# Layer 0 of a two-layer encoder trunk: recurrence products over 65 columns and rows, solves of two head pairs at once, heads in turn, another order

## Chip, cores and metric

The kernel runs on one core of one Trainium2 chip. The metric is the time of one execution in microseconds of the device: the median of three runs.

## The reference, cut to what matters

512 tokens of 1024 features pass two layers. Layer 0 projects the normed input once and feeds a convolution branch (31 taps per channel, then a layer norm) and a branch of 16 heads with a recurrence; both are gated, joined and projected. Layer 1 is a sparse attention with 16 heads. The change is in layer 0. Per head and token:

```
sa    = state @ (-kk)
state = state * w + outer(sa, kk * a) + outer(v, k)      # 64 x 64
y     = state @ r
```

## The kernel before, in words

Everything is float32. A dense product is made from two parts per operand: ScalarE copies a weight tile to `wh` (rounded), a subtraction gives the rest `wl`, and TensorE makes three passes (`dense`, line 361). The subtraction is `low` (line 331). It is issued in two halves of 128x512 per weight tile, on VectorE for the steps in a list in that line, else on GpSimd. Weights have two buffers (`st`, `wh`, `wl`).

Two heads form a pair `h` = 0 to 7 on the 128 partitions. Time is cut into 8 chunks of 64 tokens. A pair passes these steps, each a function, which `ORDER` (line 39) names with the pair's number:
- D: three dense products k, r, v. P (`hp_prep`): decay, norms. G (`hp_gate`): the gate's dense product.
- O (`hp_ops`): the operands `LTR`, `LT2`, `BK`; the key-by-query products of line 502 (64 rows of the array per head, one head's four chunks after the other's), masked on VectorE (lines 509 to 512) into `TT`; transposes. It writes the diagonal 32x32 blocks of `TT` to DRAM (`td`).
- S (`hp_solve`): reads these blocks back as 32 matrices, four copies each, on the 128 partitions (`TA`); 31 steps of two dependent VectorE operations (lines 568 and 570) make the inverses in `En`; ScalarE reorders them (line 572), transfers on its queue bring them to `TT`.
- T (`hp_solve2`): 32x32 products complete the inverse of 64x64 (lines 588 to 601).
- C (`hp_chain`): the recurrence over the 8 chunks. Per chunk: px from the state (line 612), ScalarE's copy (617), the second half of px through `TT` (619), py's first term (622), VectorE's copy into `SV` (638), py's second term and the new state's product (641, 644), VectorE's sum with the decayed state (647), ScalarE's copy of the output (649). Each line is two matmuls in the code, which are four on the engine, since a float32 product takes two passes. The products use 64 columns of the array; those of 619 and 622 use 64 rows too.
- N (`hp_norm`): group norm and gate; the result goes to DRAM.

Other steps fill in: V (convolution: two dense products, then 31 dependent operations of line 708 on VectorE), A (gate of the convolution branch), M (columns of the conditioning), rot, lora. At the end of layer 0 stand ln, Y, Z (inputs of the output projection), E and F (its two parts), W (last weights).

`LTR`, `LT2`, `TT`, `SV` have two buffers, so O of pair h waits for C of pair h - 2. The framework's scheduler makes each engine's instruction order from the order of the steps and an offset of priority per step (`PRIO`, line 47); engines then run in order. Layer 1 has its own order `ORDER1` (line 56).

Of the kernel before, what the change touches and what calls it, by code (L numbers as in the profile page):

```python
# [46 lines left out]
PRIO = {"conv": -2815, "0D": -284, "0N": -92, "1k": 123, "1v": 2526, "1K": -1011, "1w": -386, "1x": -48, "1e": 66, "0T": 91, "0S": 158, "w": 20, "0Y": -679, "0Z": 37, "0M": -30, "0F": -1121, "0lora": 459}  # L47
# [3 lines left out]
b0 x0 g1 g2 a0 h0 a1 g3 b1 h1 z0.1 x4 z0.2 z0.0 x5 a2 b2 h2 z0.3 h3 h4 z1.0  # L51
x6 h5 x7 z1.1 z1.2 z1.3 a3 z2.2 b3 z2.1 h6 h7 z2.0 z2.3 z3.0 z3.3 z3.2 z3.1
# [15 lines left out]
def trunk(ctx: ExitStack, tc: tile.TileContext, x, c, positions, ada_w, ada_b, norm_g, final_g,  # L68
# [407 lines left out]
    def hp_ops(h, o):  # L476
# [17 lines left out]
        for half in range(2):  # L494
            cs = slice(half * 4, half * 4 + 4)
            pm = []
            for hh in range(2):
                pm_ = pps([P, 4, 2, 64], "pm")
                rr = slice(64 * hh, 64 * hh + 64)
                for j in range(4):  # L500
                    cix = half * 4 + j
                    T.matmul(pm_[:, j], lhsT=BK[rr, cix], rhs=LTR[rr, 0, cix], start=True, stop=True)  # L502
                pm.append(pm_)
                if 0:

                    A.activation(TT[0:32, hh, cs], pm_[0:32, :, 0], AF.Copy)
                    A.activation(TT[32:64, hh, cs, 32:64], pm_[32:64, :, 0, 32:64], AF.Copy)
                else:
                    V.tensor_tensor(out=TT[:, hh, cs], in0=pm_[top, :, 0], in1=bc(top, 0), op=OP.mult)
# [3 lines left out]
        td = dr.tile([2, NC_, 2, 32, 32], F32, tag="td", bufs=2, name="td")  # L513
# [39 lines left out]
        return dict(LTR=LTR, LT2=LT2, TT=TT, bo=bo, td=td, W=W, SV=SV)  # L553

    def hp_solve(H):

        TA = pr.tile([P, 32, 32], F32, tag="TA", bufs=2, name="TA")
        E_ = pr.tile([P, 32, 8], F32, tag="En", bufs=2, name="En")
        G.memset(E_, 0.0)
        for m in range(4):  # L560
            r_ = slice(32 * m, 32 * m + 32)
            nc.scalar.dma_start(TA[r_], H["td"].rearrange("h c b s t -> (h c b) s t"))
            G.memset(E_[r_].rearrange("p s t -> p (s t)")[:, 8 * m:256:33], 1.0)
        for j in range(31):
            n, m = 31 - j, j // 4 + 1
            tmp = pr.tile([P, 128], F32, tag="tmp", bufs=1, name="tmp")
# [4 lines left out]
        ET = TA.rearrange("p s t -> p (s t)")[:, 0:256].rearrange("p (t s) -> p t s", s=32)  # L571
        A.activation(ET, E_.rearrange("p s t -> p t s"), AF.Copy)
        ed = dr.tile([2, NC_, 2, 8, 4, 32], F32, tag="ed", bufs=2, name="ed")
        for m in range(4):
            nc.scalar.dma_start(ed.rearrange("h c b t m s -> m (h c b) t s")[m], ET[32 * m:32 * m + 32])
        TT = H["TT"]
        for b in range(2):
            nc.scalar.dma_start(TT[32 * b:32 * b + 32, :, :, 32 * b:32 * b + 32],
                                ed[:, :, b].rearrange("h c t m s -> (t m) h c s"))
# [23 lines left out]
    def hp_chain(H):  # L603

        SV, W, LTR, LT2, TT = (H[n] for n in ("SV", "W", "LTR", "LT2", "TT"))
        Y = pr.tile([P, 4, P], F32, tag="Y", bufs=2, name="Y")
        G.memset(SV[0:64, 0], 0.0)
        hs = [(n, slice(n * 64, n * 64 + 64)) for n in range(2)]
        for c_ in range(NC_):
            px = cps([64, 2, P], "px")  # L610
            for n, s_ in hs:
                T.matmul(px[:, 0, s_], lhsT=LTR[:, n, c_, 0], rhs=SV[:, c_, s_], start=True, stop=True)
            X0 = pr.tile([64, P], F32, tag="X0", bufs=2, name="X0")
            if 0:
                V.tensor_copy(X0, px[:, 0])
            else:
                A.activation(X0, px[:, 0], AF.Copy)
# [17 lines left out]
            if 0:
                A.activation(SV[0:64, c_], px[:, 1], AF.Copy)
            else:
                V.tensor_copy(SV[0:64, c_], px[:, 1])  # L638
            for n, s_ in hs:
                l2 = LT2[:, n, c_].rearrange("p a t -> p (a t)")  # L640
                T.matmul(py[64:128, s_], lhsT=l2[:, 64:128], rhs=SV[:, c_, s_],  # L641
                         start=False, stop=True, skip_group_check=True)
                if not last:
                    T.matmul(py[0:64, s_], lhsT=l2[:, 0:64], rhs=SV[:, c_, s_],
                             start=True, stop=True, skip_group_check=True)
# [151 lines left out]
    D_, H = [None] * 8, [None] * 8  # L797
# [43 lines left out]
    def ln_stats():  # L841
# [121 lines left out]
    def ops(h):  # L963
# [3 lines left out]
        lora=lora, rot=rotary, D=dense_h, P=lambda h: hp_prep(h, D_[h]), O=ops, S=lambda h: hp_solve(H[h]),  # L967
# [308 lines left out]
```

## Time and profile before

| | |
|---|---|
| three runs | 1384.49, 1386.48, 1380.78 us (median 1384.49) |
| the profiled execution | 1381.09 us, span 1379.2 us |
| TensorE busy in the span (PE) | 1238.6 us, 90% |
| VectorE (DVE) | 1087.6 us, 79% |
| ScalarE (ACT) | 546.8 us, 40% |
| GpSimd (POOL) | 435.5 us, 32% |
| granted TensorE clock, mean | 0.918 |

A busy TensorE is not one at its peak: matmuls are pipelined and their ends overlap, so the distance between starts tells what one costs. Layer 0 ends at about 885 us.

### The profile page before, as it was taken

Reading aid. Unit: us, or ns where it says so; the run is one execution under the profiler, and the core shown is the slowest. Engines: PE = TensorE matmul, PEld = TensorE weight load, DVE = VectorE, ACT = ScalarE, POOL = GpSimd, SP = SyncE. Lnnn points to the kernel's source line nnn. Section 1 sums busy time; section 2 is a strip of 40 time slices with the busy share of each in tenths; the row PEclk is TensorE's granted clock in tenths of the full one; section 3 lists DMA queues with packets and bytes.
Section 4 is the critical chain, followed back from the end, with each engine's and each line's share of the span. In section 5 each row is a group of like instructions: output and inputs, shape, how many; then the busy total and the mean of one; then the engine's idle time right before and its main releaser. Section 6 shows DMA issues by size and latency. Waiting matters only on the chain.

```text
span 1379.2 us, 19650 instructions
## 1 busy us (share of the span) xinstructions
PE 1238.6 (90%) x6976; PEld 943.0 (68%) x6976; DVE 1087.6 (79%) x2316; ACT 546.8 (40%) x1151; POOL 435.5 (32%) x456
## 2 busy tenths in 40 slices
PE   5988888998999989989988979888989799999997
PEld 3766656766666756667556758776777588888886
DVE  4779997579798998899675863557999999966963
ACT  4433332243234333332243422445544266634643
POOL 3254332344334354444134210342455302010000
PEclk9999988779999999898596989899999899999999
DMA  9632233213122231214263774273344512133032
GB/s 297 209 109 67 79 96 100 58 51 93 48 66 69 60 93 40 73 46 113 88 195 121 244 230 130 84 199 93 115 138 122 157 44 76 55 100 106 17 92 77
DMA packets 202952, 146.51 MB, mean 106 GB/s; under 512 B 33981, under 2 KB 172646, under 8 KB 202854
## 3 DMA queue, kind: packets, MB, share of 16 engines
q1 hardware_dynamic: 159424, 111.20, 27.0%
q10 hardware_dynamic: 43430, 34.05, 9.3%
q8 instruction: 55, 0.90, 0.3%
q14 instruction: 43, 0.35, 0.1%
HBM read 119.27 MB, written 19.92 MB: 101 GB/s over the span
## 4 chain that ended last, share of the span: by engine, by line
PE 32%; DVE 13%; DMA 3%; issue 3%; ACT 2%; POOL 2%; ACTq 1%; POOLq 0%; DVEq 0%
PE pO L1175 3%; PE pl L1146 3%; DVE sc L1093 3%; DVE m L1092 2%; DVE sc L1084 2%; PE pt L1160 2%; DMA xs<-xa 1%; DMA at<-in_ada_w 1%; PE za3x L361 1%; PE zo8q5x L361 1%; POOL vs L855 1%; DVE cacc L708 1%; PE y18x L361 1%; PE zb6x L361 1%; PE zo0q7x L928 1%
## 5 line engine op out<-in xcount | busy, mean ns | idle before, releaser
L331 POOL TENSOR_TENSOR wl<-st,wh 128x512 fp32r<-128x512 f32 x170 | 240.5, 1428 | 439.6 <-ACT wh L347 388.5
L347 ACT ACTIVATE wh<-st 128x512 fp32r<-128x512 f32 (+2 forms) x256 | 147.9, 607 | 195.6 <-issue 20.3
L708 DVE SCALAR_TENSOR_TENSOR cacc<-u,PT,cacc 128x512 f32<-128x512 f32 x240 | 196.8, 827 | 0.7
L570 DVE TENSOR_TENSOR En<-En,tmp 128x60 f32<-128x60 f32 (+24 forms) x248 | 88.0, 355 | 1.6
L633 POOL TENSOR_TENSOR sw<-SV,W 64x128 f32<-64x128 f32 x56 | 47.6, 855 | 128.3 <-DVE SV L647 75.2
L331 DVE TENSOR_TENSOR wl<-st,wh 128x512 fp32r<-128x512 f32 (+3 forms) x86 | 54.6, 654 | 33.6 <-ACT wh L347 33.5
L568 DVE TENSOR_TENSOR tmp<-TA,En 128x60 f32<-128x60 f32 (+24 forms) x248 | 79.5, 320 | 1.6
L649 ACT ACTIVATE Y<-py 64x128 f32<-64x128 f32 x64 | 17.6, 274 | 121.8 <-DVE SV L647 101.4
L638 DVE COPY SV<-px 64x128 f32<-64x128 f32 x64 | 17.9, 280 | 52.6 <-PE px L619 42.1
L1155 ACT ACTIVATE lm<-lm,mx 128x512 f32<-128x512 f32 x64 | 46.0, 720 | 29.3 <-DVE mx L1154 29.1
L641 PEld LDWEIGHTS py<-SV,LT 128*64 128x64 f32 x256 | 22.0, 151 | 44.5 <-DVE SV L638 25.4
L1162 ACT ACTIVATE pth<-pt 128x512 fp32r<-128x512 f32 x64 | 37.7, 595 | 28.0 <-PE pt L1160 20.8
L641 PE MATMUL py<-SV,LT 128*64 128x64 f32 x256 | 31.4, 252 | 17.2 <-DVE SV L638 17.0
L1163 DVE TENSOR_TENSOR ptl<-pt,pth 128x512 fp32r<-128x512 f32 x64 | 43.5, 687 | 3.6 <-ACT pth L1162 3.4
L731 DVE SCALAR_TENSOR_TENSOR ac<-at,cond,ac 128x512 f32<-128x512 f32 x42 | 35.5, 845 | 12.5 <-DMA at<-in_ada_w 12.2
L1152 DVE CUSTOM_DVE_ANT_0 lm<-pl,pen 128x512 f32<-128x512 f32 x64 | 43.1, 682 | 1.4 <-PE pl L1146 0.7
L1093 DVE MATCH_REPLACE8 sc<-m,sc 128x512 f32<-128x512 f32 x64 | 43.0, 678 | 0.0
L1092 DVE MAX8 m<-sc 128x8 f32<-128x512 f32 x64 | 41.7, 684 | 0.1
L1238 POOL TENSOR_TENSOR s<-s,nhalf 128x2 f32<-128x2 f32 x2 | 1.4, 697 | 126.0 <-DVE s L1237 126.0
L1160 PE MATMUL pt<-ident,lm 128*128 128x128 f32 x256 | 38.6, 274 | 2.2 <-DVE lm L1157 2.1
L502 PE MATMUL pm<-LTR,BK 64*128 64x128 f32 x256 | 35.4, 317 | 4.9 <-DVE LTR L512 2.3
L502 PEld LDWEIGHTS pm<-LTR,BK 64*128 64x128 f32 x256 | 31.2, 217 | 12.3 <-issue 4.2
(1255 smaller groups left out, 3899.9 us busy)
## 6 DMA issues: line engine op xcount, KB each, us to landing
st<-in_even_w_in SPq DMA_DIRECT2D x57, 512.0 KB, 4.1
st<-in_odd_w_in SPq DMA_DIRECT2D x38, 512.0 KB, 3.8
at<-in_ada_w ACTq DMA_DIRECT2D x48, 256.0 KB, 3.9
ast<-in_ada_w SPq DMA_DIRECT2D x8, 1024.0 KB, 10.7
st<-in_odd_w_out SPq DMA_DIRECT2D x16, 512.0 KB, 4.4
st<-in_even_w_out SPq DMA_DIRECT2D x9, 512.0 KB, 4.9
TA<-td ACTq DMA_DIRECT2D x32, 128.0 KB, 2.7
yc<-cv_d SPq DMA_DIRECT2D x16, 256.0 KB, 4.4
```

The lines of the kernel that those rows point to most:

```text
L331: (V if STEP[0] in ('0E', '0F', '0N', '0W', '0Y', '1e', '1f', '1k', '1ki', '1qi', '1v', '1y') else G).tensor_tensor(out=dst, in0=src, in1= ...
L347: A.activation(wh[c_], st[c_], AF.Copy)
L361: T.matmul(z[:ncol, s_], lhsT=w_[:, k, :ncol], rhs=h_[k][:, s_], start=k == 0 and n == 0, stop=k == nk - 1 and n == 2)
L502: T.matmul(pm_[:, j], lhsT=BK[rr, cix], rhs=LTR[rr, 0, cix], start=True, stop=True)
L568: V.tensor_tensor(out=tv, in0=TA[:, j, j + 1:32, None].to_broadcast([P, n, m]), in1=E_[:, j:j + 1, :m].to_broadcast([P, n, m]), op=OP.mult)
L570: V.tensor_tensor(out=E_[:, j + 1:32, :m], in0=E_[:, j + 1:32, :m], in1=tv, op=OP.add)
L633: G.tensor_tensor(out=f2(sw), in0=f2(SV[0:64, c_]), in1=wb, op=OP.mult)
L641: T.matmul(py[64:128, s_], lhsT=l2[:, 64:128], rhs=SV[:, c_, s_], start=False, stop=True, skip_group_check=True)
L708: V.scalar_tensor_tensor(out=ac, in0=u[:, j:j + S], scalar=wcol(j), in1=ac, op0=OP.mult, op1=OP.add)
L1092: V.max(out=m8, in_=sc)
L1093: V.match_replace(out=sc, in_to_replace=m8, in_values=sc, imm_value=-3e38)
L1160: T.transpose(pt[:, sb], lm[:, sb * P:(sb + 1) * P], ident)
```

## The change

Six edits, all of layer 0 but where noted:
- `hp_chain`: each product takes 65 columns of the flattened operands (`Lf`, `Mf`, `T2`) and so writes 65 rows, of which 64 are used; contraction runs over 128 rows (`SV` whole, with the lower half of `LTR`'s second operand zeroed by ScalarE) or 65 (`X0` and `TT`, which now lies in one of two fixed tiles `TPAD` of 65 rows, the last one zero). py's two terms go to two halves of one tile; the new state's product is issued ahead of the output's.
- `hp_ops`: line 502's products alternate between the two heads.
- `hp_solve`: takes one or two pairs; with two, each matrix has two copies on the partitions and each operation twice the inverse's columns. `TA` and `En` have one buffer instead of two. The order has `S0.1`, `S2.3`, `S4.5`, `S6`, `S7`.
- `low`: the steps on VectorE are now 0A, 0D, 0E, 0F, 0G, 0N, 0V, 0Z, 1e, 1ki, 1v, 1y. New there are A, D, G, V, Z; back on GpSimd are 0W, 0Y, 1f, 1k, 1qi.
- `ya`: takes its tiles when it first runs, no longer in `ln_stats`.
- `ORDER`, `START` and `PRIO` are other ones; `ORDER1` is the same.

```diff
+lora V0 D0 P0 O0 D1 P1 D2 O1 S0.1 T0 P2 C0 T1 G0 V1 C1 V2 M0 rot D3 O2 P3 M1 O3 G1 N0 D4 S2.3 G2 V3 T2 C2 T3 V4 P4
+C3 D5 A6 N2 O4 A7 G3 P5 V6 G4 N1 O5 S4.5 T4 C4 N3 T5 V5 V7 C5 D6 A2 P6 O6 A1 S6 G5 D7 P7 O7 G6 S7 A3 N4 A0 A4 G7 T6
+N5 late ln Y0 Y3 A5 C6 Y4 N6 Y1 T7 Y5 Y2 C7 M2 Y6 E3 Z3 E5 Z0 E4 Z6 E1 Z1 E6 Z2 M3 Z7 N7 E7 E0 M5 M4 E2 Z4 Z5 W F5
+F1 F7.0 F6.1 F6.0 F2 F3 F4 F7.1 F0
...
+PRIO = {"conv": -2338, "0D": -318, "0N": 215, "1k": 121, "1K": -1779, "1w": -178, "1x": -48, "1e": 45, "0T": 363, "0S": 923, "w": 20, "0Z": 37, "0M": -32, "0P": -41, "1y": -26, "xs": 15, "0ln": -241, "0late": 272, "1m": 273, "0rot": -2, "0G": -15, "0F": 55, "0lora": 36}
+LOWV = ('0A', '0D', '0E', '0F', '0G', '0N', '0V', '0Z', '1e', '1ki', '1v', '1y')
...
-        (V if STEP[0] in ('0E', '0F', '0N', '0W', '0Y', '1e', '1f', '1k', '1ki', '1qi', '1v', '1y') else G).tensor_tensor(out=dst, in0=src, in1=hi.bitcast(F32), op=OP.subtract)
+        (V if STEP[0] in LOWV else G).tensor_tensor(out=dst, in0=src, in1=hi.bitcast(F32), op=OP.subtract)
...
+            pm = [pps([P, 4, 2, 64], "pm") for _ in range(2)]
+            for j in range(4):
+                cix = half * 4 + j
+                for hh in range(2):
+                    rr = slice(64 * hh, 64 * hh + 64)
+                    T.matmul(pm[hh][:, j], lhsT=BK[rr, cix], rhs=LTR[rr, 0, cix], start=True, stop=True)
...
+        A.activation(LTR[bot, :, :, 1], ident[bot, None, None, 0:64].to_broadcast([64, 2, NC_, 64]), AF.Copy, scale=0.0)
...
+        Hs = [H[h] for h in hs]
+        nb = 32 * len(Hs)
+        g = P // nb
+        w = 32 // g
+        TA = pr.tile([P, 32, 32], F32, tag="TA", bufs=1, name="TA")
+        E_ = pr.tile([P, 512], F32, tag="En", bufs=1, name="En")[:, :32 * w].rearrange("p (s t) -> p s t", t=w)
...
-            n, m = 31 - j, j // 4 + 1
+            n, m = 31 - j, j // g + 1
...
+        f2 = lambda t_: t_.rearrange("p (n v) -> p n v", v=64)
+        Lf, Mf = (t_.rearrange("p n c a t -> p (n c a t)") for t_ in (LTR, LT2))
+        def mm(out, L, o, rhs, s_, **k_):
+            m = min(65, L.shape[1] - o)
+            T.matmul(out[0:m, s_], lhsT=L[:, o:o + m], rhs=rhs, skip_group_check=True, **k_)
...
+                mm(px[:, 0], Lf, o2[n], SV[:, c_, s_], s_, start=True, stop=True)
...
+                mm(px[:, 1], T2, o2[n] // 2, X0[:, s_], s_, start=True, stop=True)
...
+                mm(py[:, 0], Lf, o2[n] + 64, SV[:, c_, s_], s_, start=n == 0, stop=False)
...
+                    mm(py[:, 1], Mf, o2[n], SV[:, c_, s_], s_, start=False, stop=True)
...
+                mm(py[:, 0], Mf, o2[n] + 64, SV[:, c_, s_], s_, start=False, stop=True)
```

## Rows read from the trace of the kernel before

**Rows 1.** Windows, sum of the eight recurrence stretches: us, busy us per engine
```profile
sum 281.00, PE 270.66 PEld 174.33 DVE 209.55 ACT 94.93 POOL 106.43; mean PE 33.83 PEld 21.79 DVE 26.19 ACT 11.87 POOL 13.30
```

**Rows 2.** Windows, sum of the four longest stretches between them
```profile
sum 278.00, PE 234.44 PEld 178.01 DVE 258.05 ACT 93.96 POOL 119.61; mean PE 58.61 PEld 44.50 DVE 64.51 ACT 23.49 POOL 29.90
```

**Rows 3.** Timeline, TensorE in a recurrence: start us, length us, instruction
```profile
366.83 0.39 PE L361 MATMUL zcg4x<-hhi,wh 128*128 128x512 f32 x1
367.06 0.40 PE L361 MATMUL zcg4x<-hlo,wh 128*128 128x512 f32 x1
367.38 0.45 PE L612 MATMUL px<-SV,LTR 128*64 128x64 f32 x4
367.76 0.49 PE L361 MATMUL zcg4x<-hhi,wl 128*128 128x512 f32 x1
```

**Rows 4.** Timeline, TensorE, eight transposes and the dense product behind
```profile
402.38 1.07 PE L531 MATMUL pk<-ident,BK 128*128 128x128 f32 x8
403.20 0.47 PE L361 MATMUL zv5x<-hhi,wh 128*128 128x512 f32 x1
```

**Rows 5.** Timeline, TensorE, products of the last visit of a chunk
```profile
378.94 0.22 PE L641 MATMUL py<-SV,LT 128*64 128x64 f32 x1
378.95 0.22 PE L644 MATMUL py<-SV,LT 128*64 128x64 f32 x1
379.00 0.22 PE L641 MATMUL py<-SV,LT 128*64 128x64 f32 x1
```

**Rows 6.** Timeline, TensorE, key-by-query products
```profile
305.42 1.13 PE L502 MATMUL pm<-LTR,BK 64*128 64x128 f32 x8 [0.17 <-DVE LTR L512]
```

**Rows 7.** Lines, VectorE: count | busy us, mean ns | idle before
```profile
L708 DVE SCALAR_TENSOR_TENSOR cacc<-u,PT,cacc 128x512 f32<-128x512 f32 x240 | 196.8, 827 | 0.7
L570 DVE TENSOR_TENSOR En<-En,tmp 128x60 f32<-128x60 f32 (+24 forms) x248 | 88.0, 355 | 1.6
L568 DVE TENSOR_TENSOR tmp<-TA,En 128x60 f32<-128x60 f32 (+24 forms) x248 | 79.5, 320 | 1.6
```

**Rows 8.** Tile and source views: count, ns min/median/max, first, last start
```profile
L568 DVE TENSOR_TENSOR tmp<-TA,En x248: 148/210/2426, 122.5 to 709.2; 128x60 f32<-128x60 f32 x12, 128x54 f32<-128x54 f32 x8, 128x66 f32<-128x66 f32 x8, 128x28 f32<-128x28 f32 x8
L570 DVE TENSOR_TENSOR En<-En,tmp x248: 148/214/4132, 123.2 to 709.8; 128x60 f32<-128x60 f32 x12, 128x54 f32<-128x54 f32 x8, 128x66 f32<-128x66 f32 x8, 128x28 f32<-128x28 f32 x8
...
L708 DVE SCALAR_TENSOR_TENSOR cacc<-u,PT,cacc x240: 731/743/2120, 80.1 to 663.5; 128x512 f32<-128x512 f32 x120
```

**Rows 9.** Lines, the subtractions; timeline, VectorE and GpSimd side by side
```profile
L331 POOL TENSOR_TENSOR wl<-st,wh 128x512 fp32r<-128x512 f32 x170 | 240.5, 1428 | 439.6 <-ACT wh L347 388.5 <-PE pvn L1105 21.4 <-issue 10.0
...
L331 DVE TENSOR_TENSOR wl<-st,wh 128x512 fp32r<-128x512 f32 (+3 forms) x86 | 54.6, 654 | 33.6 <-ACT wh L347 33.5
...
649.43 1.85 DVE L708 SCALAR_TENSOR_TENSOR cacc<-u,PT,cacc 128x512 f32<-128x512 f32 x1
...
649.45 5.90 POOL L331 TENSOR_TENSOR wl<-st,wh 128x512 fp32r<-128x512 f32 x4 [1.55 <-ACT wh L347]
```

**Rows 10.** Windows of Rows 2, line 570 alone, then line 331 alone
```profile
sum 278.00, DVE 56.10; mean DVE 14.03
...
sum 278.00, DVE 0.00 POOL 76.36; mean DVE 0.00 POOL 19.09
```

**Rows 11.** Waits, 100 to 760 us, then all: us, times, longest
```profile
POOL wl L331 <- ACT wh L347: 109.4, 30, 9.7
...
DVE wl L331 <- ACT wh L347: 33.5, 13, 10.0
```

**Rows 12.** Timeline: last chunk of C1, two solve ends, last chunk of C3
```profile
290.00 0.69 PE L612 MATMUL px<-SV,LTR 128*64 128x64 f32 x4
...
338.21 0.72 ACT L572 ACTIVATE TA<-En 128x256 f32<-128x256 f32 x1 [4.59 <-DVE En L570]
...
394.25 0.67 ACT L572 ACTIVATE TA<-En 128x256 f32<-128x256 f32 x1 [1.72 <-DVE En L570]
...
445.68 0.45 PE L612 MATMUL px<-SV,LTR 128*64 128x64 f32 x4
```

More of the change, by code (lines that the diff above doesn't have):

```diff
@@ L495, in hp_ops @@
             cs = slice(half * 4, half * 4 + 4)
-            pm = []
-            for hh in range(2):
[L498 to L509, printed above, removed]
+            pm = [pps([P, 4, 2, 64], "pm") for _ in range(2)]
[4 more added lines that the diff above has]
+                    T.matmul(pm[hh][:, j], lhsT=BK[rr, cix], rhs=LTR[rr, 0, cix], start=True, stop=True)
+            for hh in range(2):
+                pm_ = pm[hh]
+                V.tensor_tensor(out=TT[:, hh, cs], in0=pm_[top, :, 0], in1=bc(top, 0), op=OP.mult)
             for hh in range(2):
@@ L570, in hp_solve @@
             V.tensor_tensor(out=E_[:, j + 1:32, :m], in0=E_[:, j + 1:32, :m], in1=tv, op=OP.add)
-        ET = TA.rearrange("p s t -> p (s t)")[:, 0:256].rearrange("p (t s) -> p t s", s=32)
+        ET = TA.rearrange("p s t -> p (s t)")[:, 0:32 * w].rearrange("p (t s) -> p t s", s=32)
         A.activation(ET, E_.rearrange("p s t -> p t s"), AF.Copy)
[L573 to L579, printed above, removed]
+        ed = dr.tile([len(Hs), 2, NC_, 2, w, g, 32], F32, tag=f"ed{len(Hs)}", bufs=2, name="ed")
+        for m in range(g):
+            nc.scalar.dma_start(ed.rearrange("p h c b t m s -> m (p h c b) t s")[m], ET[nb * m:nb * m + nb])
+        for p_, H_ in enumerate(Hs):
+            TT = H_["TT"]
+            for b in range(2):
+                nc.scalar.dma_start(TT[32 * b:32 * b + 32, :, :, 32 * b:32 * b + 32],
+                                    ed[p_, :, :, b].rearrange("h c t m s -> (t m) h c s"))
     def hp_solve2(H):
@@ L603, in hp_chain @@
     def hp_chain(H):
-        SV, W, LTR, LT2, TT = (H[n] for n in ("SV", "W", "LTR", "LT2", "TT"))
+        SV, W, LTR, LT2, T2 = (H[n] for n in ("SV", "W", "LTR", "LT2", "T2"))
         Y = pr.tile([P, 4, P], F32, tag="Y", bufs=2, name="Y")
@@ L608, in hp_chain @@
         hs = [(n, slice(n * 64, n * 64 + 64)) for n in range(2)]
+        f2 = lambda t_: t_.rearrange("p (n v) -> p n v", v=64)
[3 more added lines that the diff above has]
+            T.matmul(out[0:m, s_], lhsT=L[:, o:o + m], rhs=rhs, skip_group_check=True, **k_)
         for c_ in range(NC_):
-            px = cps([64, 2, P], "px")
+            last = c_ + 1 == NC_
+            o2 = [(n * NC_ + c_) * P for n in range(2)]
+            px = cps([65, 2, P], "px")
@@ L611, in hp_chain @@
             for n, s_ in hs:
[L612 to L617, printed above, removed]
+                mm(px[:, 0], Lf, o2[n], SV[:, c_, s_], s_, start=True, stop=True)
+            X0 = pr.tile([65, P], F32, tag="X0", bufs=2, name="X0")
+            A.activation(X0, px[:, 0], AF.Copy)
@@ L618, in hp_chain @@
             for n, s_ in hs:
-                T.matmul(px[:, 1, s_], lhsT=TT[:, n, c_], rhs=X0[:, s_], start=True, stop=True)
-            py = cps([P, P], "py")
+                mm(px[:, 1], T2, o2[n] // 2, X0[:, s_], s_, start=True, stop=True)
+            py = cps([65, 2, P], "py")
             for n, s_ in hs:
-                T.matmul(py[64:128, s_], lhsT=LTR[0:64, n, c_, 1], rhs=SV[0:64, c_, s_],
-                         start=n == 0, stop=False, skip_group_check=True)
-            last = c_ + 1 == NC_
+                mm(py[:, 0], Lf, o2[n] + 64, SV[:, c_, s_], s_, start=n == 0, stop=False)
@@ L635, in hp_chain @@
[L635 to L638, printed above, removed]
-            for n, s_ in hs:
[L640 to L645, printed above, removed]
+                G.tensor_tensor(out=f2(sw), in0=f2(SV[0:64, c_]), in1=wb, op=OP.mult)
@@ L646, in hp_chain @@
+            V.tensor_copy(SV[0:64, c_], px[0:64, 1])
+            if not last:
+                for n, s_ in hs:
+                    mm(py[:, 1], Mf, o2[n], SV[:, c_, s_], s_, start=False, stop=True)
+            for n, s_ in hs:
+                mm(py[:, 0], Mf, o2[n] + 64, SV[:, c_, s_], s_, start=False, stop=True)
             if not last:
-                V.tensor_tensor(out=SV[0:64, c_ + 1], in0=py[0:64], in1=sw, op=OP.add)
+                V.tensor_tensor(out=SV[0:64, c_ + 1], in0=py[0:64, 1], in1=sw, op=OP.add)
@@ L795, in rotary @@
             nc.scalar.dma_start(tab_d[n, 0], r)
-    D_, H = [None] * 8, [None] * 8
+    D_, H, TD = [None] * 8, [None] * 8, [None]
+    TPAD = []
+    for n in range(2):
+        t_ = pr.tile([65, 2 * NC_ * 64], F32, name=f"T2{n}")
+        G.memset(t_[64:65], 0.0)
+        TPAD.append(t_)
     X = {}
```

50 lines of the change are left out of this document (20 added, 30 removed).

## The prediction

> **What bounds the kernel now.** I read the sums by stretch first, because the share of the whole span hides which engine is late where. Layer 0 alternates between two kinds of stretch. While a head pair's recurrence runs, eight stretches of 281 us together, TensorE is busy 270.7 us (96%) and VectorE 209.6 [rows 1]. In the four longest stretches between them, 278 us, VectorE is busy 258.1 us (93%) and TensorE 234.4; GpSimd has 119.6 [rows 2]. So a TensorE saving counts in the first kind, a VectorE saving in the second, and neither counts everywhere.
>
> Then TensorE in order of time, inside a recurrence. Dense products of 512 columns follow each other at 0.23 us (366.83, 367.06). The next instruction after 367.06 is a visit of four recurrence products (128 rows by 64 columns of the array); it begins 0.32 us later, and the dense stream resumes at 367.76 [rows 3]. From 367.06 to 367.76 is 0.70 us; less the dense product's own 0.23, a visit of four costs 0.47. Products that use the full array do not pay this: eight transposes start at 402.38 and the dense product behind them at 403.20, 0.10 us each [rows 4]. The difference is what happens when the used part of the array changes and changes back.
>
> Last VectorE. A solve's operation has a median of 0.21 us but a mean of 0.32 and 0.36; a convolution step 0.74 against 0.83 [rows 7, 8]. One such case: a convolution step takes 1.85 us beside four GpSimd subtractions in a row [rows 9]. The means are long where GpSimd works on SBUF.
>
> **The change, part by part.** The sum is made against the profiled execution, 1381.09 us (span 1379.2); the median of the three runs is 3.4 us more, which I add at the end.
>
> *A. Recurrence products over 65 columns and rows.* The number of products stays: per chunk four for px, four for its second half, four for py's first term, eight at the end. All now take the full array, so the change of shape goes. Price of one product of 65 columns: spacing inside a visit of 64 columns is 0.06 us (378.94 to 379.00 [rows 5]), that of 128 columns 0.10 [rows 4]; four cost 0.24 to 0.41 instead of 0.47. Since 65 lies next to 64 I take 0.30, with some left for entering, a saving of 0.17; about a quarter of the visits follow each other directly and pay one change less, so 0.15. Three visits per chunk, 64 chunks: 192 x 0.15 = 29 us. The fourth visit loses: its products now run two at once, each L644 0.01 us behind its L641 [rows 5], so eight cost about 4 x 0.06 + 0.24 for the change of shape = 0.48, and in the full array 8 x 0.07 = 0.56; 64 x 0.08 = 5 us. A = -24 us. Bounds: 192 x 0.23 = -44 with nothing lost at the fourth visit; 192 x 0.06 = -12 with 0.10 a product there (0.80 for 0.48, +20), so +8. It counts in full, since TensorE is 96% busy there.
>
> The Trainium skill's page TensorEngine Tiling (Array Packing), section Performance Considerations, advises the opposite of this edit: take row or column tiles where a dimension is 64 or less, and let them run together. Rows 5 do show the two running together; by that rule alone A would be the lost pairing without the saved changes, +20 us at most. The same page's Key Properties say that a change of tiling mode drains the engine, which rows 3 show as 0.32 for 0.23, and I go by those.
>
> *B. Heads in turn in L502.* The two heads lie in different rows of the array. Eight products of one head take 1.13 us [rows 6]; the 256 make 32 such groups, 36 us. If two heads ran wholly side by side, half of it would go: 0 to -18. No row shows it; each product is two passes on the same rows, and these follow each other, so I take a third, -6.
>
> *C. VectorE.* Solve: 31 x (0.210 + 0.214) = 13.1 us per head pair without disturbance, 105 us for eight. Two pairs at once: the same 62 operations, with 92 instead of 50 elements on average (counted from the loop). From 8 elements (the minimum, 0.148) to about 50 (the median) is 1.5 ns per element [rows 8], so 0.27 each, 17 us; three of these and two singles are 77. That is -28, of which 64% (56.1 of L570's 88.0 us) lies in the VectorE-bound stretches [rows 7, 10]: -18.
> Subtractions for the split weights move from GpSimd to VectorE for the steps A, D, G, V, Z: 16 + 42 + 16 + 32 + 8 = 114, at 0.68 us [rows 9], +78 us; half of them lie in the VectorE-bound stretches (76.4 us of GpSimd at 1.43 each, 53 of them [rows 10]): +39.
> The same move takes away the disturbance: (355 - 214) x 248 = 35.0, (320 - 210) x 248 = 27.3 and (827 - 743) x 240 = 20.2 us [rows 7, 8]. Some of it comes from other GpSimd work that stays, but I leave out the other lengthened VectorE lines, and set these two equal. 64% of the first two and half of the third: -50, bounded by 0 and -50 plus a tenth. C = -18 + 39 - 50 = -29 us; with the disturbance all left it would be +21.
> The Trainium skill's Perfetto Trace Analysis, section Optimizing Scalar/DVE Operations, says that a saturated VectorE may be relieved by giving work to GpSimd, and adds that the shared port may spoil this. The first half speaks against the move and gives C = +21, a rival below; rows 9 speak for the second.
>
> *D. What is added.* A subtraction in VectorE's queue must wait for ScalarE's copy of the same weights; behind it wait the solve, the convolution and the recurrence's own copies (L638, L647), and for those TensorE. GpSimd waited 109.4 us there (100 to 760 us), VectorE 33.5 us for its 86 [rows 11], 0.39 each. At that rate 57 in the VectorE-bound stretches give 22 us; VectorE has just been given slack, so I count a quarter, +6; bounds 0 and +120 (114 at 1.05).
>
> *E. Hidden.* ScalarE fills half of LTR with zeros once per head, on an engine busy 94 of 278 us [rows 2]. The solve's transfers on ScalarE's queue fall from 64 to 34. The subtractions given back to GpSimd (seven of yb and one in W, in layer 1 those of the steps k, qi and f) run where GpSimd is nearly idle, bound +-5. ORDER1 is unchanged.
>
> *F. The new order.* From C1's last chunk (290.00) to C3's (445.68) are 156 us: 48 until the other solve of the pair is off VectorE (338.21), 56 for the own solve (394.25), 51 for T3 and C3 [rows 12]. Now O3 must follow C1, one solve serves both, and then two chains of 35 us (281 / 8 [rows 1]), less A's 3 each, run one behind the other. With at least half of the 48 left for O3 and its transfers: 24 + 56 + 51 + 32 = 163, or 24 + 17 + 83 = 124 if the solve runs undisturbed. I take the middle, some 145, which A to C already contain; the ends are +7 and -32 per period, in two periods.
>
> Sum: -24 - 6 - 29 + 6 = -53; 1381.1 - 53 + 3.4 = **1332 us**.
>
> **The rivals.**
> 1. *65 columns cost like 128.* For it: no row has such a product. Against it: moving and stored columns both halve. A = +8: 1384.5 + 8 - 6 - 29 + 6 = 1364 us.
> 2. *The disturbance stays or is replaced.* VectorE takes 78 us of new work and gets nothing but the solve: C = +21, -24 - 6 + 21 + 6 = -3, 1381 us. Against it: most lengthened operations lie beside a subtraction.
> 3. *The period falls.* The solve of two pairs no longer alternates with convolution steps, and TensorE's idle time is filled by dense work: two periods of -32 and part of the same in the last pair, some -95 in all, 1290 us. For it: VectorE has 71 idle us in the recurrence stretches [rows 1] for the convolution. Against it: TensorE has no idle time there.
> 4. *Slower: VectorE's queue stands still at a subtraction.* All 114 are on the path, because the queue is in order and the recurrence's copies wait behind. Without D the sum is -59, so it decides from 59 / 114 = 0.52 us per subtraction; VectorE's rows say 0.39, GpSimd's 109.4 / 104 = 1.05. At 0.72, half way: +82, 1384.5 - 59 + 82 = 1408 us. For it: two buffers of weights, so each copy is late. Against it: today's waits of GpSimd are mostly those of an idle engine.
>
> **How the numbers follow.** The forecast 1332 (its own range 1300 to 1355) has 0.54, rival 1 0.14, rival 2 0.06, rival 3 0.16, rival 4 0.10. A difference under 0.5% (7 us) can't be told from none: rival 2 alone falls there. Faster 0.84, same 0.06, slower 0.10. The range leaves out rivals 2 and 4 and a few hundredths of rival 3's lower end: 1280 to 1376.
>
> **What would show it.** A: in the new trace the dense product behind a visit of four comes 0.5 to 0.55 us after the one ahead of it, not 0.70; at 0.70 rival 1 holds. B: sixteen L502 products in under 1.9 us, not twice 1.13. C: the solve's mean close to its median at 0.25 to 0.3 us, the convolution's at 0.74, VectorE's busy sum under 1060 us (1087.6 before); if the mean stays 0.1 above, rival 2. D: waits of VectorE's subtraction for ScalarE under 45 us; over 60, rival 4. F: fewer than 155 us from C1's last chunk to C3's; near 125, rival 3. The prediction is wrong as a whole if the recurrence stretches stay 35 us long per pair, or if they shrink and the stretches between grow by as much.

## The result, and the profile after

The kernel after takes 1317.43 us (median of four runs, 1310.96 to 1332.65), the kernel before beside it 1382.63: ratio 0.9528, 95% interval 0.9435 to 0.9621. That is 65 us less (52 to 78); 53 were forecast, and 1317 lies inside the range and the forecast's own range. One of the four runs (1332.65) was in a slower state; the other three have a median of 1312.86, and the ratio is taken from them.

The page of the profiled execution (1310.96 us): span, busy sums, then the span in 40 slices with TensorE, VectorE and the granted clock; behind it TensorE's slices of before.

```profile
span 1309.2 us, 19429 instructions
...
PE 1182.5 (90%) x6976; PEld 947.2 (72%) x6976; DVE 1019.7 (78%) x2210; ACT 554.6 (42%) x1158; POOL 310.3 (24%) x357
...
PE   6889799999999999995769989898989899999997
...
DVE  5769998899888888977676761658999999948842
...
PEclk9899898999999899995657998799999899999999
```

```profile
PE   5988888998999989989988979888989799999997
```

TensorE still fills 90% of the span, on 56 us less of busy time (1238.6 before). The new thing is the hole in slices 18 to 20, counted from 0 (590 to 690 us): digits 5, 7, 6 at a granted clock of 0.5 to 0.6. There the dense work that needs nothing from the recurrence has run out (18 dense products of 128x512 between 593 and 640 us, 155 in the like stretch of before), and TensorE waits for the last two pairs: its longest waits from 593 to 624 us are 3.9 us each for VectorE's `Y` and `En` and 4.6 for ScalarE's `yhi`.

Four windows over the recurrences, each over both chains of two pairs; then the four stretches ahead of them from 123 us on (us; busy us per engine).

```profile
sum 285.00, PE 257.41 PEld 206.46 DVE 228.10 ACT 117.70 POOL 77.11; mean PE 64.35 PEld 51.61 DVE 57.03 ACT 29.42 POOL 19.28
...
sum 312.00, PE 272.49 PEld 209.02 DVE 272.09 ACT 113.06 POOL 42.56; mean PE 68.12 PEld 52.25 DVE 68.02 ACT 28.27 POOL 10.64
```

The cut differs from [rows 1, 2], since two chains now run one inside the other. The same cut of before (191 to 291, 358 to 446, 512 to 601 and 668 to 768 us, and what lies ahead of each):

```profile
sum 377.00, PE 355.56 PEld 239.26 DVE 280.36 ACT 127.73 POOL 140.18; mean PE 88.89 PEld 59.81 DVE 70.09 ACT 31.93 POOL 35.04
...
sum 268.00, PE 224.44 PEld 171.04 DVE 253.28 ACT 90.18 POOL 114.34; mean PE 56.11 PEld 42.76 DVE 63.32 ACT 22.54 POOL 28.58
```

So the recurrences are 92 us shorter and the stretches between 44 us longer: dense work moved out of the first into the second. The trace has 597 dense products of 128x512 in the recurrences of before and 383 in those of after; in u_solve below, with the new order and single solves, it has 616. So the paired solves, which let the recurrences begin later, move it. GpSimd is busy 43 us in the stretches between, where it had 114.

The steps, each against its rows of before. TensorE in a recurrence; the first two lines are dense products at the lower clock level, the others stand at full clock (start us, length us):

```profile
203.50 0.63 PE L364 MATMUL zr3x<-hlo,wh 128*128 128x512 f32 x1
203.93 0.63 PE L364 MATMUL zr3x<-hhi,wl 128*128 128x512 f32 x1
...
207.95 0.63 PE L622 MATMUL py<-SV,LT 128*65 128x64 f32 x8
208.39 0.49 PE L364 MATMUL zr3x<-hhi,wh 128*128 128x512 f32 x1
...
363.10 0.39 PE L364 MATMUL zcg6x<-hhi,wh 128*128 128x512 f32 x1
363.32 0.40 PE L622 MATMUL px<-SV,LTR 128*65 128x64 f32 x4
363.53 0.47 PE L364 MATMUL zcg6x<-hlo,wh 128*128 128x512 f32 x1
```

The visit begins 0.22 us behind the dense product (0.32 in [rows 3]), and the next one comes 0.43 us after the one ahead (0.70 before): 0.05 us per product, with nothing left for entering. Eight products of the last visit take 0.44 us. The first two lines show the price of the clock: 0.43 us from one dense product to the next at 1.2 GHz, 0.23 at 2.4 [rows 3].

The key-by-query products (each pair has two sets of sixteen) and the last px visits of C1, C3, C5 and C7:

```profile
268.61 0.40 PE L622 MATMUL px<-SV,LTR 128*65 128x64 f32 x4
...
421.61 0.40 PE L622 MATMUL px<-SV,LTR 128*65 128x64 f32 x4
...
436.94 1.16 PE L503 MATMUL pm<-LTR,BK 64*128 64x128 f32 x16
438.03 0.51 PE L364 MATMUL zcv7x<-hhi,wl 128*128 128x512 f32 x1
...
440.75 1.90 PE L503 MATMUL pm<-LTR,BK 64*128 64x128 f32 x16
...
592.60 0.70 PE L622 MATMUL px<-SV,LTR 128*65 128x64 f32 x4 [0.38 <-DVE SV L650]
...
719.97 0.40 PE L622 MATMUL px<-SV,LTR 128*65 128x64 f32 x4
```

The same of before, beside [rows 12]:

```profile
301.75 1.71 PE L502 MATMUL pm<-LTR,BK 64*128 64x128 f32 x16
303.39 0.38 PE L437 MATMUL pc<-utri,th 128*128 128x128 f32 x1
...
600.90 0.45 PE L612 MATMUL px<-SV,LTR 128*64 128x64 f32 x4
...
767.48 0.45 PE L612 MATMUL px<-SV,LTR 128*64 128x64 f32 x4
```

A first sixteen holds TensorE for 1.09 us, where it held it for 1.64; the eight of 1.13 us in [rows 6] are half of a second set, which mostly takes longer in both kernels. From C1 to C3 are 153 us, then 171, then 127; before 156, 155 and 167. C1 itself ends 21 us earlier.

VectorE's lines and the subtractions (busy us, mean ns), the medians (ns min/median/max), and the wait of VectorE's subtraction (us, times, longest); they stand against [rows 7, 9], [rows 8] and [rows 11].

```profile
L334 POOL TENSOR_TENSOR wl<-st,wh 128x512 fp32r<-128x512 f32 x90 | 122.9, 1382 | 340.2 <-ACT wh L350 261.6
L711 DVE SCALAR_TENSOR_TENSOR cacc<-u,PT,cacc 128x512 f32<-128x512 f32 x240 | 181.4, 775 | 1.6
L334 DVE TENSOR_TENSOR wl<-st,wh 128x512 fp32r<-128x512 f32 (+2 forms) x166 | 107.4, 666 | 27.1 <-ACT wh L350 25.2
...
L575 DVE TENSOR_TENSOR tmp<-TA,En 128x126 f32<-128x126 f32 (+37 forms) x155 | 41.2, 266 | 10.6 <-DMA TA<-td 8.9
...
L577 DVE TENSOR_TENSOR En<-En,tmp 128x126 f32<-128x126 f32 (+37 forms) x155 | 39.4, 254 | 1.6
```

```profile
L575 DVE TENSOR_TENSOR tmp<-TA,En x155: 159/231/1314, 143.3 to 672.6; 128x126 f32<-128x126 f32 x9, 128x30 f32<-128x30 f32 x8, 128x56 f32<-128x56 f32 x6, 128x78 f32<-128x78 f32 x6
L577 DVE TENSOR_TENSOR En<-En,tmp x155: 156/226/1289, 144.1 to 673.5; 128x126 f32<-128x126 f32 x9, 128x30 f32<-128x30 f32 x8, 128x56 f32<-128x56 f32 x6, 128x78 f32<-128x78 f32 x6
...
L711 DVE SCALAR_TENSOR_TENSOR cacc<-u,PT,cacc x240: 732/747/1781, 81.0 to 577.8; 128x512 f32<-128x512 f32 x120
```

```profile
DVE wl L334 <- ACT wh L350: 25.2, 13, 6.9
```

Means are now close to medians: the lengthening beside GpSimd is mostly gone. The 166 subtractions now on VectorE wait no longer in all (25.2 us) than the 86 did (33.5).

### The profile page after: what moved, and what is told of

The parts are those of the page before. It is cut to its first block, busy times and chain, and to the rows that moved or that the text cites. A ratio compares the mean times of both kernels' runs of the same rounds, so it can differ in the third digit from the quotient of the medians.

```text
span 1309.2 us, 19429 instructions
## 1 busy us (share of the span) xinstructions
PE 1182.5 (90%) x6976; PEld 947.2 (72%) x6976; DVE 1019.7 (78%) x2210; ACT 554.6 (42%) x1158; POOL 310.3 (24%) x357
## 4 chain that ended last, share of the span: by engine, by line
PE 46%; DVE 21%; issue 7%; DMA 4%; POOL 3%; ACT 2%; ACTq 0%; POOLq 0%; DVEq 0%
PE py L622 3%; PE pO L1185 3%; PE pl L1156 3%; DVE sc L1103 3%; DVE m L1102 2%; PE px L622 2%; DVE cacc L711 2%; PE pt L1170 2%; DVE wl L334 2%; DVE sc L1094 2%; DMA at<-in_ada_w 2%; PE pm L503 1%; PE pss L943 1%; PE p L607 1%; PE zo8q3x L364 1%
## 5 line engine op out<-in xcount | busy, mean ns | idle before, releaser
L334 POOL TENSOR_TENSOR wl<-st,wh 128x512 fp32r<-128x512 f32 x90 | 122.9, 1382 | 340.2 <-ACT wh L350 261.6
L711 DVE SCALAR_TENSOR_TENSOR cacc<-u,PT,cacc 128x512 f32<-128x512 f32 x240 | 181.4, 775 | 1.6
L334 DVE TENSOR_TENSOR wl<-st,wh 128x512 fp32r<-128x512 f32 (+2 forms) x166 | 107.4, 666 | 27.1 <-ACT wh L350 25.2
L622 PEld LDWEIGHTS py<-SV,LT 128*65 128x65 f32 x480 | 41.6, 157 | 23.1 <-DVE SV L643 17.3
L622 PE MATMUL py<-SV,LT 128*65 128x64 f32 x480 | 47.6, 247 | 9.2 <-DVE SV L643 9.1
L575 DVE TENSOR_TENSOR tmp<-TA,En 128x126 f32<-128x126 f32 (+37 forms) x155 | 41.2, 266 | 10.6 <-DMA TA<-td 8.9
L577 DVE TENSOR_TENSOR En<-En,tmp 128x126 f32<-128x126 f32 (+37 forms) x155 | 39.4, 254 | 1.6
L622 PEld LDWEIGHTS px<-SV,LTR 128*65 128x65 f32 x256 | 25.8, 157 | 16.5 <-DVE SV L650 11.5
L1185 PE MATMUL pO<-pth,vrh 128*128 128x256 f32 x128 | 37.1, 290 | 0.0
L1042 DVE TENSOR_TENSOR sw<-sw,sn 128x512 f32<-128x512 f32 x22 | 17.0, 771 | 25.0 <-DMA sw<-qz 12.9
```

The source lines that it names most:

```text
L334: (V if STEP[0] in LOWV else G).tensor_tensor(out=dst, in0=src, in1=hi.bitcast(F32), op=OP.subtract)
L622: T.matmul(out[0:m, s_], lhsT=L[:, o:o + m], rhs=rhs, skip_group_check=True, **k_)
L711: V.scalar_tensor_tensor(out=ac, in0=u[:, j:j + S], scalar=wcol(j), in1=ac, op0=OP.mult, op1=OP.add)
L1185: T.matmul(PO[h][:, n2 * 256:n2 * 256 + 256], lhsT=a_[:, vs_], rhs=b_[:, sb], start=sb == 0 and n == 0, stop=sb == 3 and n == 2)
```

## The experiments

The question: are the steps of the sum addends? Two sets answer it: one edit taken out of the kernel after (names with u), and one put alone into the kernel before (a; a_both puts in two). One table holds all readings of stages. It is worked out from the first and last px product of each two pairs, the first product of layer 1, and the windows' sums. "Idle" is length less TensorE's busy time, from 123 us to C7's last product; tail is from there to layer 1. Each row is one profiled execution. Those of the kernels with a are from a chip on which before's median was 1374 us and not 1383, so that differences under some 10 us are not firm.

| kernel | ratio to before | recurrences | between | idle | tail | layer 1 |
|---|---|---|---|---|---|---|
| before | 1 | 377 | 268 | 65 | 110 | 501 |
| after | 0.953 | 285 | 312 | 67 | 99 | 490 |
| a_cols | 0.999 | 352 | 280 | 90 | 116 | 498 |
| a_low | 0.996 | 393 | 247 | 73 | 110 | 498 |
| a_both | 0.963 | 342 | 248 | 61 | 111 | 498 |
| a_order | 1.019 | 391 | 279 | 83 | 115 | 490 |
| u_cols | 1.012 | 360 | 304 | 75 | 108 | 493 |
| u_low | 1.015 | 316 | 364 | 113 | 102 | 492 |
| u_solve | 0.949 | 354 | 224 | 55 | 117 | 491 |

**u_cols**: the recurrence of before in the kernel after. With the columns, the new state's product goes back behind the output's; no run parts the two.

```diff
-                mm(px[:, 0], Lf, o2[n], SV[:, c_, s_], s_, start=True, stop=True)
+                T.matmul(px[:, 0, s_], lhsT=LTR[:, n, c_, 0], rhs=SV[:, c_, s_], start=True, stop=True)
...
```

> The changed kernel with the recurrence products back to 64 columns (and 64 rows where they had them); order, solves, subtractions and heads in turn stay. Terms of the forecast added up: term A comes back, 1317 + 24 = 1341 us. If the columns carry most of the gain (four products cost 0.23 us less per visit in the new trace, 192 visits): 1317 + 45 = 1362. If the new order carries it: under 1325.

Measured 1397.3 us, ratio 1.0119 (1.0057 to 1.0181): some 80 us over after, all of the gain and more. The recurrences take 75 us more, the stretches between 8 less. Windows of the first two recurrences (us, busy us per engine, granted clock, DMA share, GB/s), u_cols and then after:

```profile
199.00:306.00 107.00, 99.56 (x592) 68.51 (x590) 62.80 (x125) 32.25 (x75) 22.77 (x22) 0.68 0.23 66
389.00:483.00 94.00, 89.14 (x562) 60.88 (x560) 57.47 (x112) 25.76 (x64) 17.15 (x21) 0.70 0.12 33
```

```profile
193.00:269.00 76.00, 71.95 (x604) 57.09 (x601) 64.81 (x129) 37.22 (x80) 21.13 (x22) 0.91 0.34 101
355.00:422.00 67.00, 65.87 (x568) 52.35 (x569) 56.82 (x111) 26.05 (x65) 17.39 (x23) 0.95 0.21 59
```

About as many products take 31 and 27 us longer, and the granted clock is 0.68 and 0.70 instead of 0.91 and 0.95. A mean of 0.68 between the two levels is 64% of the time at the lower one; over the four recurrences that makes 205 us at 1.2 GHz in u_cols and 80 in after. If TensorE limited all of it, half of the 125, some 62 us, is the clock's share of the 75; that is an upper bound. So in this order the old recurrence pays twice, in the visits and in the clock, and the second part stood in no step of the forecast.

That the columns by themselves bring the clock down is not shown. In the order of before, a stretch with 64 columns ran at full clock and one with 65 at 0.77, with TensorE busy 95% of both (before, then a_both; columns as above):

```profile
358.00:446.00 88.00, 83.75 (x628) 56.42 (x624) 72.76 (x156) 28.90 (x70) 36.26 (x40) 1.00 0.23 65
...
178.00:259.00 81.00, 77.14 (x556) 61.41 (x555) 61.13 (x165) 29.28 (x68) 13.50 (x24) 0.77 0.33 93
```

**u_low**: the subtractions' list of before in the kernel after.

```diff
-LOWV = ('0A', '0D', '0E', '0F', '0G', '0N', '0V', '0Z', '1e', '1ki', '1v', '1y')
+LOWV = ('0E', '0F', '0N', '0W', '0Y', '1e', '1f', '1k', '1ki', '1qi', '1v', '1y')
```

> The changed kernel with the weights' subtractions on the engines they had before (those of A, D, G, V, Z on GpSimd again). Terms added up: +50 of disturbance, -39 of VectorE's work, -6 of waits, about 1322 us, and the solve's mean again 0.1 us above its median. If the disturbance of VectorE is the main thing: 1350 or more. If VectorE's added 78 us weigh more than the disturbance: under 1317.

Measured 1403.22 us, ratio 1.0146 (1.0092 to 1.0199): some 86 over after. Its lines of VectorE (count, busy us, mean ns, idle before):

```profile
L711 DVE SCALAR_TENSOR_TENSOR cacc<-u,PT,cacc 128x512 f32<-128x512 f32 x240 | 216.4, 909 | 2.4
L575 DVE TENSOR_TENSOR tmp<-TA,En 128x126 f32<-128x126 f32 (+37 forms) x155 | 53.6, 346 | 5.8 <-DMA TA<-td 4.3
L577 DVE TENSOR_TENSOR En<-En,tmp 128x126 f32<-128x126 f32 (+37 forms) x155 | 52.8, 340 | 1.8
```

VectorE has 80 subtractions fewer and each other line is longer: convolution 909 ns for 775, solve 346 and 340 for 266 and 254. The stretches between grow by 52 us and the recurrences by 31.

The lengthening stays where GpSimd's subtractions run and goes where they go, in every pair of kernels here: the convolution's mean is 827 to 909 ns with the list of before (before, a_cols, a_order, u_low) and 750 to 775 with the new one. The trace of before shows it by single instructions too. The 42 convolution steps that overlap a GpSimd subtraction take 1.15 us on average, the 137 that overlap no GpSimd instruction 0.74, and none of these over 0.76; the solve's operations take 0.95 to 0.97 us in the first case and 0.20 in the second. The Trainium skill, page SBUF — State Buffer, section SBUF: two separate sides, says that VectorE and GpSimd share a pair of ports that one instruction holds to its end. The trace agrees in this: the step is not slowed evenly, but from 732 ns at least to 1.78 us at most in after and 2.12 in before [rows 8].

**u_solve**: single solves in the kernel after, with two buffers again.

```diff
-D1 P1 D2 O1 S0.1 T0 ... D4 S2.3 G2 ... O5 S4.5 T4
+D1 P1 D2 O1 S0 S1 T0 ... D4 S2 S3 G2 ... O5 S4 S5 T4
```

> The changed kernel with one head pair per solve in all eight (two buffers for the solve's tiles, as before). Terms added up: 18 us of VectorE in its own stretches, 1335. If the pairing decides the time because a solve is on the path between two chains: 1350 to 1370, with longer periods from C1 to C3. If it costs what it gives, because the pair has to wait for both heads: 1317 or less.

Measured 1312.27 us, ratio 0.9485 (0.9429 to 0.9541), against 0.9528 (0.9435 to 0.9621): no loss. The solve's lines:

```profile
L575 DVE TENSOR_TENSOR tmp<-TA,En 128x60 f32<-128x60 f32 (+24 forms) x248 | 57.5, 232 | 0.5
L577 DVE TENSOR_TENSOR En<-En,tmp 128x60 f32<-128x60 f32 (+24 forms) x248 | 56.5, 228 | 0.8
```

That is 114.0 us of VectorE against 80.6 with pairs. Pairing saves the 33 us, and they are worth nothing: a single solve of the first pair of two ends earlier and its recurrence starts earlier (184 us for 193, 321 for 355, 453 for 531), while a double one keeps both waiting.

**u_turn**: one head's four products after the other's, in the kernel after.

```diff
-            for j in range(4):
-                cix = half * 4 + j
-                for hh in range(2):
+            for hh in range(2):
+                for j in range(4):
```

> The changed kernel with one head's key-by-query products after the other's. Terms added up: +6, 1323 us; from the new trace, where sixteen in turn take 1.16 us against twice 1.13, up to 16 x 1.1 = 18 us on TensorE, 1335 if TensorE is the bound wherever they stand. If these products are hidden behind VectorE: 1317.

Measured 1322.13 us, ratio 0.9568 (0.9517 to 0.9618): 5 us over after, which these runs can't tell from nothing.

**a_cols**: the recurrence over 65 columns alone, in the kernel before (the edit of `hp_chain`, `TPAD` and the zeros).

> The kernel before with the recurrence products over 65 columns and rows alone. If the terms of the forecast add: 1383 - 24 = 1359 us. If columns and subtractions need each other (VectorE stays late when only TensorE is relieved; taking either out of the changed kernel cost 80 and 86 us): 1375 or more. If the columns carry the gain by themselves, as the 80 us say: about 1305.

Measured 1372.07 us beside 1373.87, ratio 0.999 (0.9942 to 1.0038): nothing. Windows' sums, recurrences and then between:

```profile
sum 352.00, PE 311.53 PEld 244.23 DVE 288.84 ACT 130.24 POOL 137.70; mean PE 77.88 PEld 61.06 DVE 72.21 ACT 32.56 POOL 34.42
...
sum 280.00, PE 230.36 PEld 178.76 DVE 254.26 ACT 95.51 POOL 108.19; mean PE 57.59 PEld 44.69 DVE 63.56 ACT 23.88 POOL 27.05
```

The recurrences do lose 25 us, 377 to 352, which is the forecast's A. The stretches between, where VectorE is busy 254 of 280 us, give 12 back and the tail 6; TensorE's idle time rises from 65 to 90. TensorE is busy 44 us less in the recurrences (311.5 for 355.6), and even they shorten by 25 only.

**a_low**: the new list of subtractions alone, in the kernel before (the diff of u_low the other way).

> The kernel before with the subtractions' new engines alone. If the terms add: 1383 - 11 + 6 = 1378 us. If the two need each other: 1375 or more, with VectorE's operations at their medians but TensorE's visits at 0.7 us as before. If the subtractions carry the gain by themselves, as their 86 us say: about 1300.

Measured 1366.79 us, ratio 0.9961 (0.9926 to 0.9997). Lines of VectorE from 60 to 770 us:

```profile
L708 DVE SCALAR_TENSOR_TENSOR cacc<-u,PT,cacc 128x512 f32<-128x512 f32 x240 | 178.3, 756 | 0.9
...
L570 DVE TENSOR_TENSOR En<-En,tmp 128x60 f32<-128x60 f32 (+24 forms) x248 | 57.4, 232 | 0.5
L568 DVE TENSOR_TENSOR tmp<-TA,En 128x60 f32<-128x60 f32 (+24 forms) x248 | 55.2, 223 | 0.3
```

The lengthening is gone here too (827, 355 and 320 ns in [rows 7]), and the stretches between lose 21 us. The recurrences take 16 more, and all of it is in the fourth. The first three, where TensorE is busy 96%, take 272 us for 277. The fourth (642 to 763 us) takes 121 for 100: in it TensorE waits 18.7 us for the transfer that brings a solve's inverses to `TT` and 12.8 for VectorE's copy into `SV`. It is not more dense work, 575 products in the four recurrences for 597.

**a_order**: the new `ORDER`, `START` and `PRIO` and the edit of `ya`, with columns, subtractions, solves and turns of before.

> The new order and priorities alone: 64 columns, subtractions on the engines of before, single solves, one head after the other. If the terms add with the order at nothing: 1383 us. If the order was worth much by itself: under 1365. If it only fits the lighter engines: 1400 to 1480, more than either removal alone (1397, 1403).

Measured 1399.3 us, ratio 1.0192 (1.0116 to 1.0268): slower. Layer 0 ends 30 us later than before; layer 1 takes 490 us instead of 501. All five kernels of the table with the new priorities take 490 to 493 there, the other four 498 to 501, whichever list of subtractions they have. So layer 1's gain goes with the new orders and priorities; of these `PRIO` alone names steps of layer 1, but it was not run alone.

**a_solve**: paired solves alone, in the order of before.

```diff
- ... S2 M1 G2 T2 C2 G1 O3 D4 S3 ... S4 N1 D5 G3 P5 ... S5 T4 C4
+ ... M1 G2 T2 C2 G1 O3 D4 S2.3 ... N1 D5 G3 P5 ... S4.5 T4 C4
```

> The kernel before with paired solves alone, each at the place of the pair's second solve. If the terms add: 1383 - 18 = 1365 us. If the pairing is worth nothing in itself, as its removal (0.4% faster, inside the noise) says: 1375 to 1390, or slower, because the first head of a pair waits for the second.

Measured 1443.41 us (1.0235 to 1.0567 of before). Inconclusive: in this order T2 and C2 stand ahead of the double solve, so pair 2's recurrence does not wait for its solve and works on matrices that are not inverted. Its time says nothing on pairing; u_solve does.

**a_both**: columns and subtractions in the kernel before, in its order, with single solves.

> The kernel before, in its own order, with the products over 65 columns and the new list of VectorE's subtractions together; single solves, heads not in turn. Each of the two alone moved it by -0.1% and -0.4%. Theory 1 (the new order is what lets either count: in the order of before the next solve or the next pair's operands are late anyway): 1355 to 1375 us, ratio 0.985 to 1.00. Theory 2 (the two need each other, because one shortens the stretches bound by TensorE and the other those bound by VectorE, and the order adds little): 1315 to 1335 us, ratio 0.955 to 0.97. Between them, near 1345, both hold in part.

Measured 1323.68 us, ratio 0.963 (0.9577 to 0.9684), on the same chip as the two alone (before 1374.47 and 1373.87). Sums, recurrences and then between:

```profile
sum 342.00, PE 299.52 PEld 238.17 DVE 277.86 ACT 126.00 POOL 99.83; mean PE 74.88 PEld 59.54 DVE 69.47 ACT 31.50 POOL 24.96
...
sum 248.00, PE 229.38 PEld 179.26 DVE 228.74 ACT 99.91 POOL 35.58; mean PE 57.34 PEld 44.81 DVE 57.18 ACT 24.98 POOL 8.89
```

The two need each other. The recurrences lose 35 us (columns alone: 25; subtractions alone: 16 gained), the stretches between 20 (12 gained; 21), and TensorE's idle time stays at 61. With the columns alone VectorE is late in the stretches between; with the subtractions alone TensorE is in three recurrences, and the chain of the last pairs in the fourth. That these limits are why the two help each other is argued from the stages; the times show only that they do: -0.1% and -0.4% become -3.7%. What after has beyond a_both is 5 us in layer 0 and 8 in layer 1.

**c_tail, c_tail2, c_fw**: can the hole from 590 us be filled? All have single solves. c_tail moves pair 6 from E to F, so that E no longer waits for C6.

```diff
-        part(n, 8, 15, xs_d[0], t)
+        part(n, 8, 14, xs_d[0], t)
...
-        for k in range(9):
+        for k in range(10):
```

> The kernel after with single solves, and pair 6 moved from the first part of the output projection (E: now pairs 0 to 5) to the second (F: now the convolution branch and pairs 6 and 7); the order sets Z4, Z5, E7, E0, E2 a little earlier. The work is the same. Theory 1 (from about 590 us TensorE waits for the last two pairs, and E for pair 6 behind C6): E's 144 products of about 33 us run before C7 ends, instead of 684 to 754, and layer 1 starts 20 to 30 us earlier, at 790 to 800 us; 1283 to 1295 us, ratio 0.93 to 0.937. Theory 2 (the tail is bound by VectorE or by the weights' transfers and copies, which F needs in any order): within 8 us of 1312 us.

Measured 1325.49 us, ratio 0.9654 (0.9587 to 0.9722): not faster. E ends at 720 us, but F does not follow. TensorE:

```profile
719.64 0.40 PE L364 MATMUL zo8q2x<-yhi,wl 128*128 128x512 f32 x1
732.19 1.87 PE L737 MATMUL pmc<-ones_m,ac 128*128 128x1 f32 x8 [12.15 <-DVE ac L734]
...
750.63 0.79 PE L939 MATMUL zo0q5x<-hhi,wh 128*128 128x512 f32 x1 [15.20 <-ACT wh L350]
```

F's weights had been asked for behind W, whose copies need space that the last pair still holds, with both buffers of `st` taken. c_tail2 asks for two of F's weights ahead of W and moves M2 and M3.

```diff
-M2 E3 Z3 ... Z1 E6 Z2 M3 Z7 E7 E0 Z4 E2 Z5 Y6 N7 M5 M4 W F5
+E3 Z3 ... Z1 E6 Z2 E7 Z7 E0 Z4 E2 Z5 M3 Y6 U5 U1 N7 M5 M4 W F5      # M2 ahead of late; U: weights of F
```

> As c_tail, where E ended at 720 us but F's products began only at 751, because the weights of F were asked for behind W, whose copies wait for the last pair's tiles with both buffers of st taken; and where M2's tiles, in the rotation that E's xa uses, held E's results back. Here the weights of F5 and F1 are loaded ahead of W, M2 is issued ahead of late, M3 behind E. Theory 1 (with those two waits gone, TensorE's idle time ahead of layer 1 shrinks, as the pair's chain no longer decides): F begins at 722 to 738 us, layer 1 at 800 to 812 us, 1292 to 1306 us, ratio 0.935 to 0.948. Theory 2 (the transfers of the weights and of the conditioning's columns, or VectorE with the convolution branch's norm, are late in any order): F's first nine products may begin earlier but its end stays, layer 1 at 818 to 830 us, 1312 to 1325 us.

Measured 1308.12 us, ratio 0.9481 (0.9405 to 0.9557): 17 us less than c_tail, so waits of this kind were what held it; which of the moved steps counted most was not run. F begins at 712 us, but layer 1 only at 816 (818 in u_solve): between 725 and 745 F waits for the convolution branch's norm, which VectorE does late. c_fw moves F's weights alone.

```diff
-E2 Z4 Z5 W F5
+E2 Z4 Z5 U5 U1 W F5
```

> The kernel after with single solves, and the weights of F5 and F1 asked for ahead of W, nothing else: E keeps pair 6, all other steps keep their place. Theory 1 (the place of F's weights behind W costs the start of F in any order): F's first product, at 735 us with single solves alone, comes at 727 to 730 us, right behind E, and layer 1 at 808 to 812 instead of 818; 1300 to 1307 us, ratio 0.941 to 0.945. Theory 2 (with E ending only at 727, its weights and the convolution branch's norm are late by as much): within 5 us of single solves alone, ratio 0.945 to 0.952. The gain of c_tail2 over c_tail would then lie in E's early end together with the weights.

Measured 1311.77 us, ratio 0.9588 (0.953 to 0.9645), F at 733 and layer 1 at 816 us: nothing gained. Of the versions run, the medians of u_solve, c_tail2 and c_fw are 1312, 1308 and 1312 against 1317 of after; the ratios' intervals overlap, so none is shown to beat it. A comparison across chips has its own limit: u_solve and c_fw have the same median within 1 us, and ratios 1% apart, for the runs of before beside them differ too (1382.48 and 1372.64).

## Why the prediction was right, point by point

The forecast of 1332 us and the direction hold. Rivals 2 and 4 fall by the lines of VectorE and the wait of 25.2 us; rival 1 by the spacing of 0.05 us. The result lies between the forecast and rival 3, and the steps were not all right:

- **A, mis-sized.** A visit saves 0.27 us, not 0.17, and the last visit of a chunk, forecast to lose 0.08, takes 0.44 for the 0.48 counted there. The price of entering that the trace showed was the right mechanism. What failed is "It counts in full, since TensorE is 96% busy there": 192 visits at 0.27 would be 52 us, a_cols has 25 of them in the recurrences and nothing at the end. The clock, which differs between u_cols and after, stood in no step; between before and after it is no gain of the recurrences, whose mean granted clock, weighted by length, is 0.86 in both.
- **B** is of its size or less: a first sixteen takes 1.09 us for 1.64, and 5 us at the end can't be told from none. Its start, 1.13 us for every eight, was read from a slow group: an undisturbed sixteen of before takes 1.64 and not 2.26.
- **C, the lengthening: right.** Forecast 62 us for the solve's two lines and 20 for the convolution, counted over all stretches; 167.5 to 114.0 (u_solve) and 196.8 to 175.0 were measured. The subtractions' line grows by 53 us, from 54.6 to 107.4.
- **C, the solve: wrong in its worth.** The 28 us were saved on VectorE (33 measured), but the -18 did not come: u_solve, without pairing, is as fast. The step that failed put all of an engine's saving in a stretch on the path, when the wait for two pairs' operands takes its place.
- **D** held: 25.2 us of waits, under the 45 named.
- **E** held for ScalarE, no row shows it late. The +-5 for the subtractions given back hid 8 to 11 us in layer 1, which go with the new priorities.
- **F, mis-sized.** 153 us from C1 to C3, not 145; the two later periods are 171 and 127. Of some 70 us between the two profiled executions 21 came before C1's end and 39 in the last period, the second lost 16, and the tail and layer 1 gave 11 each. Rival 3's place was in part right, the last period (127 for its 124), but not its mechanism: TensorE's idle time was not filled (67 us for 65), and u_solve has the time without paired solves.
- **The sum.** The forecast added A to D as if each counted where its engine was the bound. By its own terms the columns are -24 and the subtractions -5; alone they were -2 and -7 in the medians, together -51. That the total was near is in part luck: the mutual help of columns and subtractions and the gain of layer 1 were missing, and the solve's -18 was counted.

The Trainium skill's page TensorEngine Tiling (Array Packing), section Performance Considerations, would have kept the small products. Here a_both against a_low and u_cols against after show that the full array is better for products that stand singly between dense ones. The drain that its Key Properties name agrees with the 0.27 us per visit at full clock. How much of u_cols's 80 us is that and how much the granted clock is not settled.

## What to carry to other kernels

Where two engines take turns as the bound, price a saving on one of them with the other as it is: alone it can be given back in other stretches, and here only both together shortened the whole. Try the parts of a change both alone and taken out; if these disagree, the terms are not addends. Halving the operations of a chain by handling two items at once helps the engine, not the end, when the first item then waits for the second.

## What the runs showed of the hardware beyond what was expected

In the order after, the granted clock differed with the recurrence's form. With products of 64 columns it was 0.68 and 0.70 in the first two recurrences of u_cols, with 65 columns 0.91 and 0.95 in after, at TensorE busy 93% to 98% in all four windows. Over the whole span it is 0.885 against 0.923. In the order of before the form does not decide it: the recurrences' mean by length is 0.86 in before and 0.84 in a_low with 64 columns, 0.92 in a_cols and 0.85 in a_both with 65. In the hole from 593 to 640 us, where TensorE waits, it is 0.50 in after. What makes it fall in u_cols, where TensorE is as busy, stays open.
